# Up projections of the second layer's FFN: seven half-size products per chunk in place of eight, with sums of weights on POOL

## The chip, the cores and the metric

The kernel runs on 1 core of one Trainium2 chip. The metric is the device time of one execution in microseconds (us). The kernel before takes 1777.14 us (median of 3 runs, 1777.07 to 1779.08).

## What is computed

The program is a two-layer diffusion backbone on 512 latent and 256 context tokens. Each layer ends with a channel mixer (ConvGLU). The change concerns that of the second layer, which works on the 512 latent tokens only, in float32:

```python
def conv_ffn(h, w_up, conv_w, conv_b, w_down):
    gate, val = jnp.split(jnp.dot(h, w_up), 2, axis=-1)
    return jnp.dot(jax.nn.silu(dwconv(gate, conv_w, conv_b)) * val, w_down)

x = x + gt2 * conv_ffn(modulate(rmsnorm(x, norm2_g[layer]), sh2, sc2),
                       ffn_w_up[layer], ffn_conv_w[layer], ffn_conv_b[layer], ffn_w_down[layer])
```

The model width is 1024 and `w_up` is 1024 x 5632: a gate half and a value half of 2816 each. `dwconv` is a convolution over three neighbouring tokens.

## The kernel before

Activations lie with channels on the 128 partitions and tokens along the free axis. The 2816 channels of the FFN are done in 22 chunks of 128, the 1024 input channels are 8 slices `k` of 128. To keep float32 precision, each operand is split into a rounded high part and a remainder (`split`, L37: ACT writes the high part with a cast on L42, DVE subtracts on L43), and each product is made of three TensorE passes: high x high, low x high, high x low (`fm`, L76, whose matmuls are on L85). A weight tile of 128 x 1024 comes by DMA from SP's queue (`weights`, L59, L66) and is split once.

`ffn` (L295) does, for chunk `f` (`up`): 24 matmuls of 512 columns for the gate, 24 for the value; for the first four chunks each of these is two matmuls of 256 columns, one for each half of the tokens, so that work can start when the first half of the tokens is normalised. Then ACT scales the gate (L289), DVE adds the two neighbours from PSUM (L291, L292), ACT applies Silu (L323), DVE multiplies by the value in PSUM (L325), and `split` makes `ah` and `al`. After every four chunks, `down` (L330) multiplies with `w_down`: eight output slices of 12 matmuls (L343), each added into `X` by DVE (`xupd`, L378). `up` runs one chunk ahead of `down`.

Before the FFN, `norm` (L250) normalises X in two halves of 256 tokens: squares on ACT and sums on POOL and DVE, a reciprocal root in small DVE steps (L98), then for each `k` a DVE product `u` (L275), an ACT bias into `hh` (L277), and the remainder `hl` on DVE (even `k`, L283) or POOL (odd `k`, L280 and L281).

The engines run their instructions strictly in the order in which the scheduler of the framework put them. That order is fixed when the kernel is built. Weight tiles turn through a ring of buffers (`wtile`, L47): two for raw weights (`wr`) and three for each of `wh` and `wl` in this stage.

Of the kernel before, what the change touches and what calls it, by code (L numbers as in the profile page):

```python
# [21 lines left out]
KD = 8  # L22
NF = 22
# [5 lines left out]
def f32(ap):  # L29
    return ap.bitcast(F32)  # L30


class Kernel:
    def __init__(self, tc, ins, out):
        self.tc, self.nc, self.i, self.out = tc, tc.nc, ins, out
        self.turn = {}


# [255 lines left out]

    def ffn(self, l, X, hh, hl, pool, nt, extra, swap=None, after=None):  # L295
# [1225 lines left out]
```

## Time and profile before

| | |
|---|---|
| median of 3 runs | 1777.14 us |
| the profiled execution: its time, its span | 1778.27 us, 1776.3 us |
| PE busy in the span | 1685.1 us (95%) |
| DVE, ACT, POOL busy | 1246.0, 737.0, 327.2 us |
| chain that ended last, PE's share | 69% |
| second layer's FFN, first matmul to the end of the span | 1403.9 to 1776.3 us |
| first `down` of that FFN starts (five chunks are complete) | 1466.37 us |

Times in the trace count from the start of the span. A matmul row shows how long one instruction was in flight; neighbours overlap, so the rate is read from starts, or from a stretch of the chain divided by its count. DVE, ACT and POOL rows don't overlap within an engine by more than a tenth of a us or so.

### The profile page before, as it was taken

What the parts mean: (1) busy time and instruction counts of PE and PEld (TensorE: products, weight loads), DVE (VectorE), ACT (ScalarE), POOL (GpSimd) and SP (SyncE); (2) the same over time, 40 slices, a digit from 0 to 9 for tenths busy, and PEclk for the clock granted to TensorE, in tenths of its full rate; (3) what the DMA queues carried; (4) which work ended last, traced back from release to release, by engine and by line L of the source; (5) the groups of instructions that cost most, each with busy time, mean ns of one, the idle gap of its engine ahead of it and who ended that gap; (6) DMA issues with size and microseconds to landing.
All of it is one profiled execution on the core that took longest, in us unless ns stands there. A gap on an engine that the chain in (4) does not pass through costs nothing.

```text
span 1776.3 us, 25328 instructions
## 1 busy us (share of the span) xinstructions
PE 1685.1 (95%) x9622; PEld 1443.6 (81%) x9622; DVE 1246.0 (70%) x2285; ACT 737.0 (41%) x1369; POOL 327.2 (18%) x361
## 2 busy tenths in 40 slices
PE   6798889999999999999999998999999899999998
PEld 1587787888888888888888887788888798888887
DVE  5897898988878667585867548877778854544444
ACT  3333877888243222221222225645453442332231
POOL 4824445454040000000000005112020300000000
PEclk8898999999999999999999999999998999999999
DMA  8352000003525234242523222111112223322232
GB/s 276 112 169 64 10 11 7 19 1 132 166 82 191 96 130 143 95 157 81 166 96 131 72 75 76 52 48 49 60 36 95 72 96 98 104 95 95 96 98 91
DMA packets 68317, 166.28 MB, mean 94 GB/s; under 512 B 8290, under 2 KB 30818, under 8 KB 67810
## 3 DMA queue, kind: packets, MB, share of 16 engines
q1 hardware_dynamic: 68194, 164.66, 28.2%
q8 instruction: 76, 1.25, 0.3%
q14 instruction: 45, 0.37, 0.1%
q10 hardware_dynamic: 2, 0.01, 0.0%
HBM read 160.44 MB, written 4.20 MB: 93 GB/s over the span
## 4 chain that ended last, share of the span: by engine, by line
PE 69%; DVE 13%; ACT 7%; POOL 6%; issue 3%; DMA 1%; SPq 0%; POOLq 0%; ACTq 0%; DVEq 0%
PE psS L85 30%; PE psT L343 7%; PE psU L343 7%; PE psU L85 4%; PE psR L85 3%; PE psT L85 2%; PE psO L343 2%; PE psR L343 2%; PE S L424 1%; ACT p L432 1%; PE psO L469 1%; POOL hl L281 1%; DVE junk L138 1%; PE psR L95 1%; PE state L1190 1%
## 5 line engine op out<-in xcount | busy, mean ns | idle before, releaser
L85 PE MATMUL psS<-hl,wh 128*128 128x512 f32 (+1 forms) x992 | 347.2, 351 | 4.4 <-POOL hl L281 4.3
L85 PE MATMUL psS<-hh,wh 128*128 128x512 f32 (+1 forms) x992 | 346.3, 350 | 0.4 <-ACT hh L277 0.4
L85 PE MATMUL psS<-hh,wl 128*128 128x512 f32 (+1 forms) x992 | 346.0, 349 | 0.0
L42 ACT CAST wh<-wr 128x1024 fp32r<-128x1024 f32 (+2 forms) x187 | 193.5, 1036 | 349.1 <-PE psO L343 141.3
L43 DVE TENSOR_TENSOR wl<-wr,wh 128x1024 fp32r<-128x1024 f32 (+2 forms) x187 | 229.4, 1227 | 46.5 <-ACT wh L42 46.2
L85 PEld LDWEIGHTS psS<-hl,wh 128*128 128x128 f32 x992 | 186.4, 188 | 32.9 <-POOL hl L281 7.1
L85 PEld LDWEIGHTS psS<-hh,wh 128*128 128x128 f32 x992 | 186.5, 188 | 26.6 <-ACT hh L277 0.9
L85 PEld LDWEIGHTS psS<-hh,wl 128*128 128x128 f32 x992 | 186.5, 188 | 25.4
L291 DVE SCALAR_TENSOR_TENSOR y<-psS,fcw,y 128x511 f32<-128x511 f32 (+1 forms) x60 | 39.5, 658 | 145.6 <-ACT y L289 145.6
L261 POOL TENSOR_TENSOR sa<-sa,sq 128x256 f32<-128x256 f32 (+1 forms) x18 | 18.3, 1016 | 643.7 <-ACT sq L260 643.7
L138 DVE CUSTOM_DVE_ANT_0 y<-ar,cb 128x1024 f32<-128x1024 f32 x112 | 136.4, 1219 | 0.0
L289 ACT ACTIVATE y<-psS,fcb,fcw 128x512 f32<-128x512 f32 (+1 forms) x60 | 40.3, 706 | 207.2 <-PE psS L85 207.2
L378 DVE SCALAR_TENSOR_TENSOR X<-psU,mod,X 128x512 f32<-128x512 f32 (+1 forms) x69 | 47.9, 695 | 89.4 <-PE psU L343 78.9
L435 POOL TENSOR_SCALAR p<-p,rs 128x768 f32<-128x768 f32 (+1 forms) x96 | 73.9, 776 | 114.6 <-DVE rs L434 75.4
L138 DVE CUSTOM_DVE_ANT_0 junk<-ar,cb 128x1024 f32<-128x1024 f32 x64 | 84.0, 1312 | 0.5
L343 PE MATMUL psT<-ah,wh 128*128 128x512 f32 (+1 forms) x184 | 71.6, 389 | 2.2 <-DVE X L378 1.2
L343 PE MATMUL psU<-ah,wh 128*128 128x512 f32 (+1 forms) x184 | 71.4, 388 | 1.2 <-DVE X L378 1.2
L343 PE MATMUL psU<-ah,wl 128*128 128x512 f32 (+1 forms) x184 | 71.0, 386 | 0.0
L343 PE MATMUL psT<-ah,wl 128*128 128x512 f32 (+1 forms) x184 | 71.0, 386 | 0.0
L325 DVE TENSOR_TENSOR y<-y,psS 128x512 f32<-128x512 f32 (+1 forms) x60 | 34.1, 597 | 52.5 <-PE psS L85 52.4
L343 PE MATMUL psT<-al,wh 128*128 128x512 f32 (+1 forms) x184 | 70.9, 385 | 0.0
L343 PE MATMUL psU<-al,wh 128*128 128x512 f32 (+1 forms) x184 | 70.7, 384 | 0.0
(666 smaller groups left out, 4381.9 us busy)
## 6 DMA issues: line engine op xcount, KB each, us to landing
ar<-in_ada SPq DMA_DIRECT2D x88, 512.0 KB, 3.5
wr<-in_wup SPq DMA_DIRECT2D x88, 512.0 KB, 3.5
wr<-in_wdn SPq DMA_DIRECT2D x44, 512.0 KB, 3.4
pr<-in_adak SPq DMA_DIRECT2D x16, 256.0 KB, 4.3
wr<-in_w_out SPq DMA_DIRECT2D x8, 512.0 KB, 3.6
wr<-in_w_mqk SPq DMA_DIRECT2D x8, 512.0 KB, 3.5
wr<-in_w_mv SPq DMA_DIRECT2D x8, 512.0 KB, 3.6
wr<-in_w_mo SPq DMA_DIRECT2D x8, 512.0 KB, 3.4
```

What stands on the lines that cost most here:

```text
L42: nc.scalar.copy(hi, src)
L43: nc.vector.tensor_tensor(lo, src, f32(hi), op=SUB)
L85: nc.tensor.matmul(ps, a, b[:, k, x0:x0 + n], start=i == 0, stop=i == 3 * nk - 1)
L95: nc.tensor.matmul(ps, a[:, k, t * 128:(t + 1) * 128], b, start=i == 0, stop=i == 3 * nk - 1)
L138: nc.vector.tensor_tensor_reduce(out, raw, self.cb[:, c], 1.0, 0.0, MUL, ADD, self.mraw[l][:, n, c:c + 1])
L261: (nc.vector if k % 2 else nc.gpsimd).tensor_tensor(sa[k % 2], sa[k % 2], sq, op=ADD)
L289: nc.scalar.activation(y[:, t0:t0 + n], p, AF.Identity, bias=b, scale=w[1])
L291: nc.vector.scalar_tensor_tensor(y[:, t0 + 1:t0 + n], p[:, 0:n - 1], w[0], y[:, t0 + 1:t0 + n], op0=MUL, op1=ADD)
L325: nc.vector.tensor_tensor(y[:, t0:t0 + n], y[:, t0:t0 + n], p, op=MUL)
L343: nc.tensor.matmul(ps[:, 0:n], x[:, off:off + 128], y[:, t0:t0 + n], start=m == 0, stop=m == 3 * nf - 1)
L378: self.nc.vector.scalar_tensor_tensor(X[:, o, t0:t0 + n], ps[:, 0:n], self.mod[l][:, g0 + o, c:c + 1], X[:, o, t0:t0 + n], op0=MUL, op1=ADD)
L435: nc.gpsimd.tensor_scalar(p[:, 0:nk], p[:, 0:nk], r, 1.0, op0=MUL, op1=MUL)
```

## The change

The product of weights (two halves in output channels, gate and value, by two halves in input channels) with activations (two halves in input channels by two halves of tokens) is done in Winograd's form of Strassen's scheme. With the weights' quarters A11 (gate, k 0 to 3), A12 (gate, k 4 to 7), A21 and A22 (value), it takes seven products of 128 x 512 x 256 in place of eight.

- `norm_w` (in place of `norm` for this FFN) writes seven split operands: `B11` and `B21` from the first half of the tokens, `B22` from the second, and `T1` to `T4`, which are differences of the two halves. It keeps `h` of both halves in float32. Its sums are made of pairs of slices, 512 columns each.
- For each chunk, POOL makes four sums of weights of 128 x 512 (`S12`, `S43`: S1 = A21 + A22, S2 = S1 - A11, S4 = A12 - S2, S3 = A11 - A21). ACT and DVE split them as they do raw weights. Three tiles of 128 x 1024 (`A1`, `S12`, `S43`) and one of 128 x 512 (`A22`) are split per chunk, in place of two of 128 x 1024.
- Products accumulate in PSUM: `Y` (tags T and U) takes B11, T2, T3 and T4 in turn and is read in between; `Z` and `W` share a tile. Copies `p5`, `u2` and `g` go out on ACT, sums are added on DVE. The convolution reads its gate from SBUF (`g`).
- The value product for the second half of the tokens and the remainder `al` are done on POOL.
- A chunk is a generator of five stages; `ffn_w` interleaves stages of chunk f and f + 1. `down` uses the PSUM tags R and O.
- The ring has three more raw buffers and two more each for `wh` and `wl`, in the pool of this FFN (`we`), which takes up memory that the last part of the mixer and `norm_w` used.

```diff
     def wtile(self, tag, n, cols, dt):
...
+        if self.we and tag != "wr":
+            bufs += [(self.we, tag + "e"), (self.we, tag + "f")]
+        elif self.we:
+            bufs += [(self.we, tag + x) for x in "efg"]
...
+    def norm_w(self, pool, X, l, B, half, n, kept):
...
+        def low(name, k, src, eng):
+            eng.tensor_tensor(B[name][1][:, k], src, f32(B[name][0][:, k]), op=SUB)
+
+        for k in range(KD):
+            u = pool.tile([128, n], F32, tag="u", name="u", bufs=3)
+            nc.vector.scalar_tensor_tensor(u, X[:, k, t0:t1], s[:, k, 0:1], rb[:, 0:n], op0=MUL, op1=MUL)
+            sh = self.mod[l][:, 24 + k, 0:1]
+            nc.scalar.activation(h[:, k], u, AF.Identity, bias=sh)
+            if half == 0:
+                nm, kk = ("B11", k) if k < 4 else ("B21", k - 4)
+                nc.scalar.activation(B[nm][0][:, kk], u, AF.Identity, bias=sh)
+                low(nm, kk, h[:, k], nc.gpsimd if k % 2 else nc.vector)
+        if half == 0:
+            return
+        g = kept[0]
+        k2 = [(slice(a, a + 2), slice(a + 4, a + 6)) for a in (0, 2)]
+
+        for a, b in k2:
+            nc.vector.tensor_tensor(g[:, a], h[:, a], g[:, a], op=SUB)
+            nc.scalar.copy(B["T1"][0][:, a], g[:, a])
+            low("T1", a, g[:, a], nc.vector)
+        for a, b in k2:
+            nc.scalar.copy(B["B22"][0][:, a], h[:, b])
+            low("B22", a, h[:, b], nc.gpsimd)
+            nc.vector.tensor_tensor(h[:, a], h[:, b], h[:, a], op=SUB)
+            nc.vector.tensor_tensor(h[:, b], h[:, b], g[:, a], op=SUB)
+            nc.scalar.copy(B["T2"][0][:, a], h[:, b])
+            low("T2", a, h[:, b], nc.vector)
+        for a, b in k2:
+            nc.scalar.copy(B["T3"][0][:, a], h[:, a])
+            low("T3", a, h[:, a], nc.gpsimd)
+        for a, b in k2:
+            nc.vector.tensor_tensor(g[:, b], g[:, b], h[:, b], op=SUB)
+            nc.scalar.copy(B["T4"][0][:, a], g[:, b])
+            low("T4", a, g[:, b], nc.vector)
...
+        def prod(ps, w, x, first, last):
+            wh, wl = w
+            xh, xl = x
+            m = 0
+            for k in range(4):
+                for a, b in ((wh, xh), (wl, xh), (wh, xl)):
+                    nc.tensor.matmul(ps, a[:, k], b[:, k], start=first and m == 0, stop=m == 11, skip_group_check=True)
+                    m += 1
...
+        def chunk(f):
+            rg, rv = self.raw(i["wup"][l, f, 0], KD, 128), self.raw(i["wup"][l, f, 1], KD, 128)
+            A1 = self.halves(rg, KD, 128)
...
+            prod(Y, part(A1, 0), B["B11"], True, False)
+            prod(Z, part(A1, 1), B["B21"], True, True)
+            nc.scalar.copy(g[:, 0:n], Z)
+            nc.vector.tensor_tensor(g[:, 0:n], g[:, 0:n], Y, op=ADD)
+            yield
+            S = pool.tile([128, KD, 128], F32, tag="S12", name="S12", bufs=1)
+            nc.gpsimd.tensor_tensor(S[:, 0:4], rv[:, 0:4], rv[:, 4:8], op=ADD)
+            nc.gpsimd.tensor_tensor(S[:, 4:8], S[:, 0:4], rg[:, 0:4], op=SUB)
+            S12 = self.halves(S, KD, 128)
+            prod(W, part(S12, 0), B["T1"], True, False)
+            p5 = pool.tile([128, n], F32, tag="p5", name="p5", bufs=2)
+            nc.scalar.copy(p5, W)
+            yield
+            prod(Y, part(S12, 1), B["T2"], False, False)
+            S_ = pool.tile([128, KD, 128], F32, tag="S43", name="S43", bufs=1)
+            nc.gpsimd.tensor_tensor(S_[:, 0:4], rg[:, 4:8], S[:, 4:8], op=SUB)
+            nc.gpsimd.tensor_tensor(S_[:, 4:8], rg[:, 0:4], rv[:, 0:4], op=SUB)
+            S43 = self.halves(S_, KD, 128)
...
+            nc.scalar.copy(u2, Y)
+            prod(W, part(S43, 0), B["B22"], False, True)
+            nc.vector.tensor_tensor(g[:, n:nt], u2, W, op=ADD)
+            yield
+            A22 = self.halves(rv[:, 4:8], 4, 128)
+            prod(Y, part(S43, 1), B["T3"], False, False)
...
+            nc.vector.tensor_tensor(v2, p5, Y, op=ADD)
...
+            nc.scalar.activation(y, g, AF.Identity, bias=cb[:, f:f + 1], scale=cw[:, 1, f:f + 1])
+            for t0, m in segs:
+                nc.vector.scalar_tensor_tensor(y[:, t0 + 1:t0 + m], g[:, t0:t0 + m - 1], cw[:, 0, f:f + 1],
+                                               y[:, t0 + 1:t0 + m], op0=MUL, op1=ADD)
+                nc.vector.scalar_tensor_tensor(y[:, t0:t0 + m - 1], g[:, t0 + 1:t0 + m], cw[:, 2, f:f + 1],
+                                               y[:, t0:t0 + m - 1], op0=MUL, op1=ADD)
+            nc.scalar.activation(y, y, AF.Silu)
+            nc.gpsimd.tensor_tensor(y[:, n:nt], y[:, n:nt], v2, op=MUL)
+            yield
+            prod(Y, A22, B["T4"], False, True)
+            nc.vector.tensor_tensor(y[:, 0:n], y[:, 0:n], Y, op=MUL)
...
+            nc.scalar.copy(ah, y)
+            nc.gpsimd.tensor_tensor(al, y, f32(ah), op=SUB)
...
+        def up(f):
+            if f == 0:
+                upto(0, 1)
+                upto(1, 1)
+            upto(f, 3)
+            upto(f + 1, 1)
+            if f == 0:
+                upto(f + 1, 2)
+            upto(f, 4)
+            upto(f + 1, 2)
+            upto(f, 5)
...
-                ps = self.B("TU" if c == 0 or last else "RO")
+                ps = self.B("TU" if own and (c == 0 or last) else "RO")
...
-                    self.norm(NP, X, 1, 1, gh, gl, [(256 * half, 256 * half + 256, 0)])
+                    self.norm_w(NP, X, 1, B, half, 256, kept)
```

Two places of the fixed order matter below. The first is the start of the FFN. On ACT, right after the last `hh` of the second half of the tokens (L277), there stood before the scaling of chunk 0's gate; the weights of chunks 0 and 1 had been cast earlier:

```order
L277 ACTIVATE hh_13863<-u_14167,mod1_646 128x256
L277 ACTIVATE hh_13863<-u_14171,mod1_646 128x256
L289 ACTIVATE y_14293<-psS_14183,fcb1_654,fcw1_652 128x512
L42 CAST wh_14361<-wr_14359 128x1024
```

Now there stand the casts of B22 and T1 to T4 (`Ts` holds T1, T2 and T3), and behind them the cast of chunk 0's gate weights (`wh_14208`) and of its first sums (`wh_14281`):

```order
L325 ACTIVATE h_14145<-u_14167,mod1_646 128x256
L337 CAST Ts_13871<-h_13996 128x512 x2
L340 CAST B22h_13867<-h_14145 128x512
L347 CAST Ts_13871<-h_14145 128x512
L344 CAST Ts_13871<-h_14145 128x512
L347 CAST Ts_13871<-h_14145 128x512
L351 CAST T4h_13869<-h_13996 128x512
L344 CAST Ts_13871<-h_14145 128x512
L351 CAST T4h_13869<-h_13996 128x512
L43 CAST wh_14208<-wr_14204 128x1024
L43 CAST wh_14281<-S12_14278 128x1024
```

POOL likewise makes the remainders of B22 and T3 first (`L319`) and chunk 0's sums of weights behind them; DVE splits `wl_14209` behind its last T4. PE meets this at its 13th product matmul. `psU` is the first product of chunk 1, whose weights (`wh_14245`) were split early; `psT_14212` is the first of chunk 0:

```order
L393 MATMUL psU_14249<-B11h_13863,wl_14246 128x256
L393 MATMUL psU_14249<-B11l_13864,wh_14245 128x256
L315 MATMUL psO_14142<-ident_90,nwy_14130 128x128 x2
L393 MATMUL psT_14212<-B11h_13863,wh_14208 128x256
L393 MATMUL psZ_14213<-B21h_13865,wh_14208 128x256
L393 MATMUL psZ_14250<-B21h_13865,wh_14245 128x256
```

What moved: after 12 matmuls everything on PE stands behind `wh_14208`, which stands behind the casts of T4.

The second place is a chunk of the later FFN on DVE. Before, a chunk had six instructions there:

```order
L43 TENSOR_TENSOR wl_16292<-wr_16289,wh_16291 128x1024
L43 TENSOR_TENSOR al_16212<-y_16205,ah_16211 128x512
L291 SCALAR_TENSOR_TENSOR y_16277<-psS_16215,fcw1_652,y_16277 128x511
L292 SCALAR_TENSOR_TENSOR y_16277<-psS_16215,fcw1_652,y_16277 128x511
L43 TENSOR_TENSOR wl_16322<-wr_16319,wh_16321 128x1024
L325 TENSOR_TENSOR y_16277<-y_16277,psS_16216 128x512
```

Now it has ten, of which six read two operands from SBUF (four splits, and L435 and L437, whose gate `g` was in PSUM before):

```order
L44 TENSOR_TENSOR wl_16681<-S43_16677,wh_16680 128x1024
L426 TENSOR_TENSOR g_16443<-u2_16551,psZ_16442 128x256
L435 SCALAR_TENSOR_TENSOR y_16621<-g_16443,fcw1_652,y_16621 128x511
L437 SCALAR_TENSOR_TENSOR y_16621<-g_16443,fcw1_652,y_16621 128x511
L408 TENSOR_TENSOR g_16576<-g_16576,psU_16574 128x256
L44 TENSOR_TENSOR wl_16737<-wr_16568,wh_16736 128x512
L431 TENSOR_TENSOR v2_16619<-p5_16513,psT_16441 128x256
L44 TENSOR_TENSOR wl_16704<-wr_16699,wh_16703 128x1024
L443 TENSOR_TENSOR y_16621<-y_16621,psT_16441 128x256
L44 TENSOR_TENSOR wl_16764<-S12_16760,wh_16763 128x1024
```

What moved: on each chunk L431 (`v2`) and L443, for which PE waits before it may write `Y` again, now stand behind splits of the next chunk; and POOL, which had nothing to do here, has six instructions a chunk.

## Rows read from the trace of the kernel before

**Rows 1.** The chain that ended last, in order of time: start us, us, what.

```profile
1426.66 5.76 PE psR L85 x48
...
1466.37 2.72 PE psT L343 x12
...
1488.13 43.52 PE psS L85 x192
...
1749.25 10.89 PE psS L85 x48
1760.23 0.70 DVE y L325
...
1772.43 0.75 DVE X L378
```

**Rows 2.** Busy time by stretch: us, PE, PEld, DVE, ACT, POOL, PEclk, DMA share, GB/s.

```profile
1410.00:1414.00 4.00, 3.34 (x28) 3.34 (x29) 3.22 (x13) 0.00 (x0) 0.61 (x1) 1.00 0.65 168
1414.00:1422.00 8.00, 7.53 (x59) 6.95 (x58) 5.24 (x12) 4.21 (x9) 5.44 (x8) 1.00 0.14 49
...
1488.13:1531.65 43.52, 43.52 (x193) 36.04 (x193) 20.05 (x23) 15.18 (x19) 0.00 (x0) 1.00 0.27 89
```

**Rows 3.** Line 85, weight loads for psR: duration ns min/median/max, first and last start, forms.

```profile
L85 PEld LDWEIGHTS psR<-hh,wh x88: 187/188/192, 534.2 to 1454.8; 128*128 128x128 f32 x88
```

**Rows 4.** Groups by line and shape, DVE from 1400 us: busy us, mean ns | idle.

```profile
L43 DVE TENSOR_TENSOR wl<-wr,wh 128x1024 fp32r<-128x1024 f32 x65 | 80.0, 1232 | 13.4 <-ACT wh L42 13.4
...
L43 DVE TENSOR_TENSOR al<-y,ah 128x512 fp32r<-128x512 f32 x22 | 15.0, 684 | 0.7 <-ACT ah L42 0.7
L291 DVE SCALAR_TENSOR_TENSOR y<-psS,fcw,y 128x511 f32<-128x511 f32 x20 | 15.0, 750 | 69.3 <-ACT y L289 69.3
```

**Rows 5.** The same for ACT.

```profile
L42 ACT CAST wh<-wr 128x1024 fp32r<-128x1024 f32 x65 | 68.0, 1048 | 133.5 <-PE psU L343 85.1 <-PE psS L85 42.8 <-PE psR L85 4.9
...
L277 ACT ACTIVATE hh<-u,mod 128x256 fp32r<-128x256 f32 x16 | 7.2, 500 | 8.6 <-DVE u L275 8.6
```

**Rows 6.** Two lines of POOL, each by its own view: duration ns min/median/max.

```profile
L1168 POOL TENSOR_TENSOR Dl<-D,Dh x16: 1273/1291/2292, 1142.6 to 1350.6; 128x512 fp32r<-128x512 f32 x16
...
L281 POOL TENSOR_TENSOR hl<-v,hh x24: 726/752/2115, 505.7 to 1420.2; 128x256 fp32r<-128x256 f32 x16, 128x512 fp32r<-128x512 f32 x8
```

**Rows 7.** Instructions in order of time: start us, us, engine, line, what.

```profile
35.39 1.21 DVE L138 CUSTOM_DVE_ANT_0 junk<-ar,cb 128x1024 f32<-128x1024 f32 x1
...
35.42 6.37 POOL L206 TENSOR_TENSOR X<-X,rbs 128x256 f32<-128x256 f32 x4
...
36.54 0.68 DVE L173 TENSOR_SCALAR s<-mod,n0g 128x2 f32<-128x2 f32 x1
...
37.13 1.21 DVE L138 CUSTOM_DVE_ANT_0 junk<-ar,cb 128x1024 f32<-128x1024 f32 x1
```

**Rows 8.** The same view around the second half of the norm.

```profile
1402.59 1.26 DVE L275 SCALAR_TENSOR_TENSOR u<-X,s,psO 128x256 f32<-128x256 f32 x3
...
1410.02 1.67 DVE L43 TENSOR_TENSOR wl<-wr,wh 128x1024 fp32r<-128x1024 f32 x1
...
1414.16 1.26 DVE L275 SCALAR_TENSOR_TENSOR u<-X,s,psO 128x256 f32<-128x256 f32 x3 [0.63 <-PE psO L272]
1414.67 1.31 ACT L277 ACTIVATE hh<-u,mod 128x256 fp32r<-128x256 f32 x3 [6.35 <-DVE u L275]
```

**Rows 9.** Busy time by stretch at the end of the mixer, columns as above.

```profile
1337.00:1340.00 3.00, 0.90 (x5) 0.72 (x6) 3.00 (x7) 2.23 (x4) 0.00 (x0) 0.76 0.97 415
1340.00:1344.00 4.00, 4.00 (x21) 4.00 (x20) 2.99 (x5) 0.26 (x2) 0.00 (x0) 0.50 0.32 131
1344.00:1347.00 3.00, 3.00 (x12) 2.71 (x12) 2.51 (x8) 0.26 (x1) 0.00 (x0) 0.50 0.37 126
1347.00:1350.00 3.00, 3.00 (x14) 2.72 (x14) 2.48 (x6) 2.08 (x4) 0.66 (x1) 0.70 0.02 5
```

**Rows 10.** PE in order of time in the same place.

```profile
1339.62 0.45 PE L1190 MATMUL state<-V,kwh 128*128 128x130 f32 x1 [1.48 <-DVE num L1227]
```

More of the change, by code (lines that the diff above doesn't have):

```diff
@@ L36, in __init__ @@
         self.turn = {}
+        self.we = None
     def split(self, hi, lo, src, scale=None):
@@ L292, in conv, with raw, halves @@
             nc.vector.scalar_tensor_tensor(y[:, t0:t0 + n - 1], p[:, 1:n], w[2], y[:, t0:t0 + n - 1], op0=MUL, op1=ADD)
-    def ffn(self, l, X, hh, hl, pool, nt, extra, swap=None, after=None):
+    def raw(self, src, n, cols):
+        t = self.wtile("wr", n, cols, F32)
+        self.nc.sync.dma_start(t, src)
+        return t
+    def halves(self, src, n, cols):
+        hi = self.wtile("wh", n, cols, F32R)
+        lo = self.wtile("wl", n, cols, F32R)
+        self.split(hi, lo, src)
+        return hi, lo
@@ new lines, in ffn_w, with go, upto @@
+    def ffn_w(self, l, X, B, pool, nt):
+        a = {}
+        make = self.up_w(l, B, pool, nt, a)
+        ch = {}
+        def go(f, n=1):
+            for _ in range(n):
+                next(ch[f], None)
+        stage = {}
+        def upto(f, st):
+            if f >= NF:
+                return
+            if f not in ch:
+                ch[f] = make(f)
+            while stage.get(f, 0) < st:
+                go(f)
+                stage[f] = stage.get(f, 0) + 1
+        def up(f):
[9 more added lines that the diff above has]
+            upto(f, 5)
+        self.ffn(l, X, None, None, pool, nt, [], up=up, a=a)
@@ L296, in ffn @@
+    def ffn(self, l, X, hh, hl, pool, nt, extra, swap=None, after=None, up=None, a=None):
         nc, i = self.nc, self.i
@@ L299, in ffn, with up_plain @@
         cw, cb = self.fcw[l], self.fcb[l]
-        a = {}
+        own = up is None
+        a = {} if own else a
         ytile = lambda: pool.tile([128, D], F32, tag="y", name="y", bufs=3)[:, 0:nt]
-        def up(f):
+        def up_plain(f):
             alone = f < 4 and f % 2 == 1
@@ L368, in ffn @@
             while done < min(NF, fs[-1] + 2):
-                up(done)
+                (up or up_plain)(done)
                 done += 1
@@ L1392, in build @@
             hp = tc.alloc_tile_pool(name="h3", bufs=1, reuse_waits="tile")
-            gh = hp.tile([128, KD, NL], F32R, name="hh")
-            gl = hp.tile([128, KD, NL], F32R, name="hl")
+            B = {nm: [hp.tile([128, 4, NL // 2], F32R, tag=nm + e, name=nm + e) for e in "hl"]
+                 for nm in ("B11", "B21", "B22", "T4")}
+            z = HP.tile([128, KD, T], F32R, tag="hl", name="Ts").rearrange("p k t -> p (k t)").rearrange(
+                "p (j k t) -> p j k t", j=6, k=4)
+            B.update({nm: [z[:, 2 * j], z[:, 2 * j + 1]] for j, nm in enumerate(("T1", "T2", "T3"))})
+            kept = {}
             with tc.tile_pool(name="o1", bufs=1, reuse_waits="tile") as OP, \
```

46 lines of the change are left out of this document (45 added, 1 removed).

## The prediction, made before the changed kernel ran

> **What bounds the kernel now.** I read first the chain that ended last, in order of time. In the second layer's FFN it is PE without a break: 192 matmuls of 512 columns in 43.52 us, 226.7 ns each, then the next `down` [rows 1]. The first four chunks use 256 columns, 48 in 5.76 us, 120 ns each [rows 1]. The busy time by stretch then shows what the others do meanwhile: in the stretch from 1488 us DVE is busy for 20 of 43.5 us and POOL for none, at the full granted clock [rows 2]. So PE sets the end, and less work for PE is worth its full price as long as PE finds its operands ready. Third, the start of this FFN, where PE was already fed by a chain of DVE, ACT and POOL [rows 8], yet busy for 7.5 of 8 us just before 1422 [rows 2]. Fourth, places where DVE and POOL work at once [rows 7], since the change puts much on both.
>
> **PE's work.** Before: 4 chunks x 96 x 0.120 + 18 x 48 x 0.2267 = 46.1 + 195.8 = 241.9 us. Now every chunk has 7 x 12 = 84 matmuls of 256 columns: 22 x 84 x 0.120 = 221.8 us. That is 20.1 us less, not an eighth, because a half-width matmul costs 120 ns and not 113. A weight load takes 188 ns [rows 3], though such matmuls follow each other at 120 ns: loads overlap. The Trainium skill ("TensorE: Matmul & The Clock Gate", section "The mechanism") says that loads overlap with matmuls in flight only if they go to another row group; by that each of these, on all 128 rows, would have to wait for its load, but this trace disagrees with its 120 ns.
>
> **DVE and POOL get in each other's way.** While POOL ran four sums of 128 x 256 in 6.37 us, 1.59 each [rows 7], against 0.73 alone [rows 6], DVE read two SBUF operands in its own instructions, and a DVE step on two elements took 0.68 us [rows 7]. They alternate: one DVE instruction of 1.21 us and one of POOL of 0.73 have a period of 1.74 us (35.39 to 37.13) [rows 7], 0.9 of the sum of their durations. I count a "shared" instruction (DVE with two SBUF operands, every sum on POOL) at 0.9 of its duration and let none overlap. The Trainium skill ("SBUF — State Buffer", section "Who interferes with whom") calls it an exclusive lock, held for the whole instruction. The trace agrees that one waits for the other; by the rule's letter the factor is 1.0.
>
> Shared work per chunk now, with 1.23 us for a split, 0.68 for half of one, 0.70 for a neighbour sum (between 0.68 and 0.75) [rows 4], 1.29 and 0.73 for POOL's 512 and 256 columns [rows 6]: DVE 3 x 1.23 + 0.68 + 2 x 0.70 = 5.8, POOL 5 x 1.29 + 0.73 = 7.2, in all 13.0, x 0.9 = 11.7 us. PE needs 84 x 0.120 = 10.1. So within four chunks the shared work is the longer of the two; during a `down` (21.76 us) it is the shorter and some is made in advance.
>
> **The start.** The second half's `u` steps began at 1414.16, behind two splits in DVE's queue, one of 1.67 us [rows 8]; these now stand later, but ACT has two activations per slice in place of one in the first half. I take 1411 (bounds 1410 and 1414). Eight steps paced by ACT, 0.44 each (1.31 for three [rows 8]), end at 1414.6. Then DVE has twelve shared steps of 512 columns up to the last source of T4: 12 x 0.68 = 8.2, and between them POOL's four remainders and up to two sums of weights at 1.16: 4.6 to 7. That is 1429. The cast of T4 (0.6) and then, next in ACT's order, of chunk 0's weights (1.05 [rows 5]) end at 1431; the split's second half waits behind two more steps of T2 and T4 and POOL's turns: 1433. PE has 12 matmuls until then, whose operands are ready by 1410; it stands still for over 20 us where before it was nearly full [rows 2].
>
> From 1433 to the first `down` PE has 30 products of 1.44 us (chunks 0 to 3 and three of chunk 4, one being done): 43.2 us. After a gap of some 2 us (PE idle 1.48 us before 1339.62, with three transposes just ahead of that [rows 9, 10]) the granted clock was 0.50, the 1.2 GHz level, from 1340 to 1347 and 0.70 to 1350 [rows 9]: about 9 us at half speed, 4.5 lost. Together 1480.7. The other way round, the shared work between 1428 and that `down`: DVE the two late steps 1.4, three splits and a half for chunk 0 and so on through chunk 4 (18.7), four for `w_down` 4.9, eight neighbour sums 5.6; POOL 16 sums of weights 20.6 and four times 2.02 for the value product and `al`. Sum 59.3, x 0.9 = 53.4: 1481.4. Both give 1481. Before, the first `down` began at 1466.37 [rows 1], four products of a chunk further on.
>
> **From there on.** Before, 309.9 us remained. Now: four products 5.8, 17 chunks x 10.08 = 171.4, five `down`s and a half 119.7, and the 5.2 us by which the end is longer than its matmuls: 302.1. At the very end chunk 21 has nothing beside it: PE waits for `v2`, and `al` takes 1.29 on POOL in place of 0.68 [rows 4, 6], while the product with Y is half as wide: +1.7, bounds 0 and 3. Between two `down`s the shared work is 24.9 on DVE (ten splits and three halves, four for `w_down`, eight sums) and 23.6 on POOL, 48.4 in all, x 0.9 = 43.6 against PE's 40.3. The excess is 3.3; part can slip under the first columns of the `down`, and part of PE's waits for `v2` come on top. No row shows the balance; the bounds are 0 (all made in advance) and 8.1 (factor 1.0). I take 2.5, nearer the factor that the row gives, four times: 10.
>
> **The sum.** 1481 + 302.1 + 1.7 + 10 = 1794.8 for the end of the span, against 1776.3 (the last DVE step at 1772.43 [rows 1] and the copy out behind it): +18.5 on the profiled execution's own 1778.27, so 1796.8. The median of the runs is 1.1 lower than that execution: 1795.7, and I say 1795.
>
> SP's queue carries the same bytes, with five raw buffers in place of two; the transfer for chunk 0 waits for the mixer's last matmuls, at about 1402, and lands long before 1429, so it costs nothing. ACT's added copies (three of 256 columns, one and a half casts, some 3 us a chunk) fit in its idle time (15 of 43.5 us busy [rows 2]). Clock drops inside the FFN are not counted: PE's gaps there would be short.
>
> **Rivals.**
> 1. *The two engines run side by side and PE restarts early.* For it: `u` steps that read PSUM show no slowing [rows 8]; against it, the 1.59 us sums. Without any blocking, 1414.6 + 8.2 + 1.7 + 1.2 = 1425.7, no clock loss, + 43.2 = 1468.9, + 302.1 + 0 to 1.7: 1771 to 1773, in time 1772 to 1774, faster by about 4 us. It decides if PE's first product of chunk 0 runs before 1426.
> 2. *The start costs what I say, but after it PE alone sets the pace*, with the clock up at once: 1433 + 43.2 + 302.1 + 1.7 = 1780, time 1781, or up to 3 us less with an earlier start.
> 3. *Full exclusion through every group of four chunks*, as the lock rule has it, from rows at factor 1.0: first `down` at 1430 + 59.3 = 1489, then 8.1 per group: 1489 + 302.1 + 1.7 + 32 = 1825, time 1826. The period of 1.74 us speaks against the letter of it, DVE's strict order (a late split delays `v2`, and with it PE) for it.
> 4. *Weight loads bind* at 188 ns: 22 x 84 x 0.068 = +126 us. The 120 ns rows are against it.
> That the change doesn't cut PE's work can be ruled out: 84 matmuls a chunk stand in the order.
>
> **How the numbers follow.** Forecast (1785 to 1806) 0.59; rival 2 (1777 to 1785) 0.15, a little over half of it within 0.2%; rival 1 0.10; rival 3 (1806 to 1826) 0.14; rival 4 0.02. The range from 1777 to 1813 leaves out rivals 1 and 4 and half of rival 3. About 0.2% (3.6 us) is what a measurement can tell from no change: faster 0.10, same 0.09, slower 0.81.
>
> **What would show it.** Right: matmuls of L393 starting 120 ns apart; PE idle from about 1411 until about 1430, ended by ACT's cast of `wh`; a granted clock near 0.5 for some us behind it; POOL's sums of 512 columns at 1.5 to 2.5 us and splits of DVE at well over 1.23; first `down` near 1481. Wrong: PE's gap under 15 us, POOL's sums near 1.29 with DVE busy, or gaps in later groups of over 8 us or none.

## The result, and the profile after

The changed kernel takes 1841.06 us (median of 4 runs, 1838.86 to 1846.16) against 1778.11 of the kernel before (4 runs, 1777.07 to 1779.30): ratio 1.0358, 95% interval 1.0335 to 1.0381. It is slower, as forecast, but by 63 us, not by 18, and lies outside the range. The profiled execution took 1838.86 us, its span is 1837.1 (before: 1778.27 and 1776.3).

The chain that ended last, in order of time, shows where each `down` begins (start us, us, what):

```profile
1494.16 2.52 PE psR L535 x11
...
1567.95 2.52 PE psR L535 x11
...
1641.21 2.52 PE psR L535 x11
...
1789.38 2.52 PE psR L535 x11
```

Before, five `down`s began from 1466.37 to 1727.49, 65.28 apart [rows 1]; now they are 73.8 apart. The 60.8 us of span are: first `down` 27.8 later, four groups 4 x (73.8 - 65.28) = 34.1, and from the fifth `down` on 1.1 less (47.7 against 48.8).

The 27.8 are too few by 7.4 us. The first `u` of the norm ran at 1395.18, where before it ran at 1402.59 [rows 8], behind work that the change leaves alone; the first layer's first `down` also began at 590.5 us in place of 596.1, and in the traces of all runs it begins between 590.5 and 598.4. So two traces can stand some us apart before they come to the changed code. Counted from the first `u`, the first `down` came after 99.0 us in place of 63.8, 35.2 later. Times of two traces are therefore compared below from a place that both share, where it matters.

Busy time by stretch, kernel after (us, PE, PEld, DVE, ACT, POOL, granted clock, DMA share, GB/s): three pieces of the start, one `down`, the products up to the next `down`, and four pieces around one gap.

```profile
1410.00:1418.00 8.00, 0.00 (x0) 0.00 (x0) 6.85 (x7) 2.55 (x5) 6.72 (x5) 0.50 0.00 0
1418.00:1424.00 6.00, 1.36 (x5) 1.14 (x5) 6.00 (x4) 2.98 (x5) 5.73 (x4) 0.50 0.00 0
1424.00:1430.00 6.00, 4.54 (x25) 4.46 (x25) 3.76 (x4) 0.88 (x1) 3.16 (x2) 0.58 0.28 87
1567.95:1589.60 21.65, 21.65 (x99) 17.93 (x98) 9.91 (x14) 4.31 (x5) 3.85 (x3) 1.00 0.31 90
1589.60:1641.21 51.61, 44.62 (x338) 43.30 (x337) 39.34 (x40) 25.31 (x39) 36.30 (x22) 0.93 0.26 85
1622.00:1625.00 3.00, 2.45 (x21) 2.24 (x19) 2.96 (x2) 0.54 (x2) 2.92 (x3) 1.00 0.00 0
1625.00:1628.00 3.00, 0.67 (x3) 0.67 (x4) 3.00 (x5) 1.83 (x3) 1.97 (x2) 0.83 0.01 3
1628.00:1631.00 3.00, 3.00 (x18) 3.00 (x18) 0.89 (x2) 0.64 (x1) 1.06 (x1) 0.60 0.76 225
1631.00:1634.00 3.00, 3.00 (x27) 3.00 (x27) 2.03 (x2) 2.16 (x4) 1.81 (x1) 1.00 0.36 125
```

Against [rows 2]: between two `down`s PE stands still for 7.0 of 51.6 us and has a mean clock of 0.93, where it had neither gaps nor a lower clock. In the `down` POOL works for 3.85 us only; after it for 36 of 52.

The costliest groups of DVE, kernel after, 1430 to 1760 us (busy us, mean ns | idle before); they answer to [rows 4]:

```profile
L44 DVE TENSOR_TENSOR wl<-wr,wh 128x1024 fp32r<-128x1024 f32 x34 | 55.2, 1624 | 7.0 <-ACT wh L43 6.9
L44 DVE TENSOR_TENSOR wl<-S,wh 128x1024 fp32r<-128x1024 f32 x38 | 51.5, 1354 | 28.4 <-ACT wh L43 25.9 <-PE psZ L393 1.5 <-issue 0.9
L435 DVE SCALAR_TENSOR_TENSOR y<-g,fcw,y 128x511 f32<-128x511 f32 x19 | 27.7, 1456 | 12.4 <-ACT y L433 12.4
...
L426 DVE TENSOR_TENSOR g<-u,psZ 128x256 f32<-128x256 f32 x19 | 7.8, 412 | 8.0 <-PE psZ L393 7.0 <-ACT wh L43 1.0
```

and of POOL, which answer to [rows 6]:

```profile
L411 POOL TENSOR_TENSOR S<-wr 128x512 f32<-128x512 f32 x19 | 33.4, 1757 | 20.4 <-DMA wr<-in_wup 14.9 <-DVE wl L44 5.5
...
L447 POOL TENSOR_TENSOR al<-y,ah 128x512 fp32r<-128x512 f32 x18 | 32.6, 1812 | 22.0 <-ACT ah L446 22.0
```

A split takes 1.35 to 1.62 us in place of 1.23, a neighbour step 1.46 in place of 0.75, a sum on POOL 1.53 (L420) to 1.76 (L411) in place of 1.29. L426 and DVE's other short steps, which take one operand from PSUM and one from SBUF, take 0.41, the same as where POOL does nothing (0.41 to 0.42 in e3 below).

What PE waited for between 1494 and 1760 us (total, times, longest):

```profile
PE psU L393 <- DVE y L443: 8.1, 4, 2.0
PE psU L393 <- DVE v L431: 7.4, 3, 2.9
PE psT L393 <- DVE v L431: 5.2, 4, 2.1
PE psZ L393 <- ACT g L407: 4.6, 4, 1.1
```

The first three are short steps of 0.41 us, which come late in DVE's queue. At the start (in order of time: start us, us, engine, line, what, and in brackets the idle time before it), POOL and DVE take turns in the T steps, and PE restarts on ACT's cast of chunk 0's weights:

```profile
1395.18 1.27 DVE L323 SCALAR_TENSOR_TENSOR u<-X,s,psO 128x256 f32<-128x256 f32 x3
...
1411.38 1.74 DVE L343 TENSOR_TENSOR h<-h 128x512 f32<-128x512 f32 x1 [1.15 <-POOL B22l L319]
1412.53 1.71 POOL L319 TENSOR_TENSOR Ts<-h,Ts 128x512 fp32r<-128x512 f32 x1
1413.04 1.75 DVE L342 TENSOR_TENSOR h<-h 128x512 f32<-128x512 f32 x1
...
1422.64 0.58 PE L393 MATMUL psT<-B11h,wh 128*128 128x256 f32 x1 [18.69 <-ACT wh L43]
...
1425.54 0.58 PE L393 MATMUL psT<-B11h,wl 128*128 128x256 f32 x1 [1.47 <-DVE wl L44]
```

### The profile page after: what moved, and what is told of

Read it like the earlier page. It is cut to its first block, busy times and chain, and to the rows that moved or that the text cites. A ratio compares the mean times of both kernels' runs of the same rounds, so it can differ in the third digit from the quotient of the medians.

```text
span 1837.1 us, 26989 instructions
## 1 busy us (share of the span) xinstructions
PE 1682.9 (92%) x10222; PEld 1469.5 (80%) x10222; DVE 1355.5 (74%) x2383; ACT 798.4 (43%) x1497; POOL 543.6 (30%) x485
## 4 chain that ended last, share of the span: by engine, by line
PE 60%; DVE 18%; ACT 9%; POOL 7%; issue 5%; DMA 1%; POOLq 0%; SPq 0%; DVEq 0%; ACTq 0%
PE psS L90 18%; PE psR L535 5%; PE psO L535 5%; PE psU L90 4%; DVE wl L44 4%; PE psT L535 3%; PE psU L535 3%; PE psR L90 2%; PE psT L393 2%; PE psU L393 2%; ACT wh L43 2%; PE psT L90 2%; PE S L616 2%; PE psO L661 1%; PE psZ L393 1%
## 5 line engine op out<-in xcount | busy, mean ns | idle before, releaser
L43 ACT CAST wh<-wr 128x1024 fp32r<-128x1024 f32 (+3 forms) x187 | 183.5, 985 | 290.1 <-PE psO L535 154.1
L44 DVE TENSOR_TENSOR wl<-wr,wh 128x1024 fp32r<-128x1024 f32 (+3 forms) x187 | 238.9, 1278 | 43.0 <-ACT wh L43 42.6
L90 PE MATMUL psS<-hl,wh 128*128 128x512 f32 (+1 forms) x640 | 216.7, 340 | 2.1 <-POOL hl L286 2.1
L90 PE MATMUL psS<-hh,wh 128*128 128x512 f32 (+1 forms) x640 | 216.2, 338 | 0.4 <-ACT hh L282 0.4
L90 PE MATMUL psS<-hh,wl 128*128 128x512 f32 (+1 forms) x640 | 216.2, 338 | 0.0
L90 PEld LDWEIGHTS psS<-hl,wh 128*128 128x128 f32 x640 | 120.3, 188 | 18.0 <-POOL hl L286 3.7
L90 PEld LDWEIGHTS psS<-hh,wh 128*128 128x128 f32 x640 | 120.3, 188 | 15.1 <-ACT hh L282 0.6
L90 PEld LDWEIGHTS psS<-hh,wl 128*128 128x128 f32 x640 | 120.3, 188 | 14.4
L44 DVE TENSOR_TENSOR wl<-S,wh 128x1024 fp32r<-128x1024 f32 x44 | 59.2, 1346 | 32.2 <-ACT wh L43 29.7
L619 DVE TENSOR_REDUCE nm<-S 128x1 f32<-128x768 f32 x64 | 60.2, 946 | 3.9 <-PE S L616 3.5
```

The costliest lines, as they stand in the source:

```text
L43: nc.scalar.copy(hi, src)
L44: nc.vector.tensor_tensor(lo, src, f32(hi), op=SUB)
L90: nc.tensor.matmul(ps, a, b[:, k, x0:x0 + n], start=i == 0, stop=i == 3 * nk - 1)
L619: nc.vector.tensor_reduce(nm, s[:, 0:nk], axis=AX.X, op=MAX, negate=True)
```

## Experiments

Three theories for the 8.5 us per group. **A**: DVE's instructions on two SBUF operands and POOL's exclude each other, so POOL's work lengthens DVE's queue, and what PE waits for comes late. **B**: the chain raw load, sum, split, product, with one buffer each for S12 and S43, makes the products late, whatever engine makes the sums. **C**: DVE's own added work is too much. The table has all runs; the kernel before measured 1778.1 to 1779.3 beside them. "Group" is the mean time from one `down` to the next; PE alone needs 28 x 1.44 + 21.76 = 62.1.

| run | us | ratio to before, 95% | group |
|---|---|---|---|
| the change | 1841.1 | 1.0358 (1.0335 to 1.0381) | 73.8 |
| e1_no_sums | 1794.7 | 1.0090 (1.0073 to 1.0107) | 64.4 |
| e2_sums_unread | 1849.6 | 1.0402 (1.0381 to 1.0422) | 75.1 |
| e3_no_pool | 1781.6 | 1.0016 (1.0001 to 1.0031) | 62.1 |
| e4_act_drains | 1837.7 | 1.0326 (1.0301 to 1.0352) | 71.6 |
| e5_tail_dve | 1839.1 | 1.0352 (1.0328 to 1.0376) | 72.4 |
| e6_sums_dve | 1800.7 | 1.0131 (1.0113 to 1.0150) | 65.8 |
| e8_deep | 1849.8 | 1.0408 (1.0388 to 1.0429) | 74.3 |
| e10_idle_sums | 1837.9 | 1.0323 (1.0304 to 1.0342) | 72.1 |
| e14_two_idle | 1805.0 | 1.0152 (1.0130 to 1.0175) | 66.4 |
| e11_idle_copies | 1799.2 | 1.0106 (1.0089 to 1.0124) | 65.3 |
| e12_low_dve | 1780.9 | 1.0008 (0.9997 to 1.0019) | 62.1 |
| e7_start | 1780.5 | 1.0013 (1.0002 to 1.0025) | 62.1 |
| e9_start2 | 1778.9 | 1.0000 (0.9988 to 1.0013) | 62.1 |
| e13_start3 | 1778.8 | 1.0001 (0.9988 to 1.0015) | 62.1 |

### Sums left out, and sums made but not read (e1, e2)

```diff
-            S = pool.tile([128, KD, 128], F32, tag="S12", name="S12", bufs=1)
-            nc.gpsimd.tensor_tensor(S[:, 0:4], rv[:, 0:4], rv[:, 4:8], op=ADD)
-            nc.gpsimd.tensor_tensor(S[:, 4:8], S[:, 0:4], rg[:, 0:4], op=SUB)
-            S12 = self.halves(S, KD, 128)
+            S12 = self.halves(rv, KD, 128)
```

and the same for S43 with `rg`; e2 has only the last line of it, so POOL's sums stay.

> Left out: the four sums of weights on POOL in each chunk; the splits of S12 and S43 read the raw values of rv and rg instead. Everything else, the seven products among it, stays. Measured for the changed kernel: 73.8 us from one down to the next, of which PE alone would need 62.1, and 1841 us in all. Theory A (DVE and POOL hold each other up, which stretches DVE's queue, so the PSUM reads that PE waits for come late): with only two POOL instructions left in a chunk the splits fall back from 1.55 to about 1.25 us, groups take 62 to 66 us, the start gains 4 to 8 us: 1795 to 1805. Theory B (the order of dependences: a sum is made late because its buffer or its source is late, and its split and product with it): the same fall, 1795 to 1805. Theory C (DVE's own added work, or PE's narrow products, set the pace): groups stay at 71 to 74 us, 1832 to 1843.

> POOL makes all four sums of weights as in the changed kernel, but no split reads them: the splits of S12 and S43 read the raw values of rv and rg. What is left out is the use of the sums, and with it the chain sum, split, product. Theory A (the two engines hold each other up while both work): the sums still run beside DVE, so groups stay at 71 to 75 us and the time at 1825 to 1843. Theory B (the chain through the sums makes the products late): groups fall to 62 to 66 us and the time to 1795 to 1805, as without sums.

Without sums 1794.7, about what A and B both said, so C is out; with sums that no split reads 1849.6. So it is not the chain through the sums: cutting it gave nothing, taking POOL's work away gave 46. That e2 is 8.6 slower than the change, and above A's range as well, stays unexplained. In e2 DVE's splits are at least as slow as in the change (groups of DVE, 1430 to 1760 us):

```profile
L44 DVE TENSOR_TENSOR wl<-wr,wh 128x1024 fp32r<-128x1024 f32 x71 | 119.3, 1700 | 25.9 <-ACT wh L43 23.7 <-PE psZ L393 2.0
```

One part of B is left in e2: POOL still reads the raw weights and so holds their buffers. The run with useless sums below takes that away too.

### All of POOL's work on DVE (e3)

```diff
-            nc.gpsimd.tensor_tensor(S[:, 0:4], rv[:, 0:4], rv[:, 4:8], op=ADD)
+            nc.vector.tensor_tensor(S[:, 0:4], rv[:, 0:4], rv[:, 4:8], op=ADD)
```

and so for the other three sums, for `y` times `v2` and for `al`.

> The four sums, the product y times v2 and the remainder al of each chunk run on DVE; POOL does nothing in the chunks. The result is the same. Theory A: DVE's instructions return to the lengths they have alone (split 1.23, sum of 512 columns 0.68, of 256 about 0.35 to 0.40), so DVE needs 5.8 + 4 x 0.68 + 0.68 + 0.4 + four PSUM steps of about 0.4 = 11.2 us a chunk against PE's 10.1, less than the 11.7 at factor 0.9 and the longer real one: groups of 66 to 70 us, time 1808 to 1828, faster than the changed kernel by 13 to 33 us although DVE does more. Theory B (the chain through the sums, whatever engine makes them): groups 72 to 76, 1835 to 1850. Theory C (DVE's own work is the bound, POOL relieves it): DVE gets 3.8 us more per chunk, groups 80 to 88, 1870 to 1900.

1781.6 us: 59.5 less than the change, better than A's range (1808 to 1828), and less than e1, which does 88 instructions fewer. The groups are PE's alone: the `down`s come 62.06 apart. The chain, then the stretch between two of them, then DVE's groups from 1430 to 1760 us:

```profile
1485.45 2.75 PE psR L535 x12
...
1547.51 2.75 PE psR L535 x12
...
1609.57 2.75 PE psR L535 x12
```

```profile
1569.30:1609.40 40.10, 40.10 (x336) 39.93 (x336) 37.96 (x59) 24.94 (x39) 0.00 (x0) 1.00 0.30 93
```

```profile
L44 DVE TENSOR_TENSOR wl<-S,wh 128x1024 fp32r<-128x1024 f32 x44 | 53.7, 1220 | 8.9 <-ACT wh L43 8.8
...
L435 DVE SCALAR_TENSOR_TENSOR y<-g,fcw,y 128x511 f32<-128x511 f32 x21 | 15.7, 745 | 0.0
...
L420 DVE TENSOR_TENSOR S<-wr,S 128x512 f32<-128x512 f32 x22 | 15.1, 687 | 0.3
```

All of DVE's instructions have their lengths of before, and PE has no gap and the full clock. B and C fall: the chain is the same and DVE has more to do. DVE works for 38.0 of 40.1 us between two `down`s. In the change it worked for 39.3 of 51.6, with 40 instructions in place of 59: giving a third of its instructions to POOL had relieved DVE of nothing. A sum takes 0.69 on DVE and 1.29 on POOL by itself [rows 6]; if only one of them can run at a time, POOL is no help but the dearer place.

### One part moved alone (e5, e6)

In e5 the tail (`y` times `v2`, `al`) goes to DVE and the sums stay on POOL; in e6 the other way round.

> Only the tail of a chunk (y times v2, 256 columns, and the remainder al, 512 columns) goes from POOL to DVE; the four sums of weights stay on POOL. The same result. If the instructions that exclude each other simply add up and set the pace between two downs (changed kernel: 5.8 us on DVE and 7.2 on POOL per chunk by their durations alone, 13.0, four times 52.0, and 52.1 us measured between the end of one down and the next), then a chunk has 5.8 + 0.68 + 0.42 + 4 x 1.29 = 12.06, and a group takes 21.7 + 48.2 = 70 us, 3.8 less than 73.8: 1841 - 4 x 3.8 - 3 = 1823, bounds 1817 to 1829. If only the number of POOL's sums and their late sources matter (order, buffers), groups stay at 73 to 75 us: 1834 to 1846.

> The other part: the four sums of weights go to DVE, y times v2 and al stay on POOL. The same result. By the same addition a chunk has 5.8 + 4 x 0.68 = 8.5 on DVE and 2.02 on POOL, 10.5 in all, so 42.2 between two downs against PE's 40.3: groups of 62 to 65 us, and 1781 (all on DVE) + 4 x 2 + 2 = 1791, bounds 1783 to 1798. If what counts is that PE's next product waits for DVE alone, whose queue now holds the sums too: groups of 70 us and more, 1820 to 1840.

e6 came out just above its upper bounds (1800.7, bound 1798; groups 65.8, bound 65): two instructions per chunk left on POOL still cost 19 us against e3. What PE waits for there, 1494 to 1760 us:

```profile
PE psT L393 <- DVE v L431: 7.8, 8, 1.3
PE psU L393 <- DVE v L431: 1.8, 4, 0.5
```

The chain that ended last in e6 also runs through POOL's product itself (L440, 3.08 us from 1605.17), so e6 alone doesn't part the exclusion from the chain through the tail.

e5 is a miss: groups fell by 1.4, not by 3.8, and the time by 2 us, less than the runs of either kernel spread. Adding up durations alone doesn't give the pace (more on this below).

### PE freed from DVE's late steps (e4), and more raw buffers (e8)

```diff
-            nc.vector.tensor_tensor(v2, p5, Y, op=ADD)
+            t3 = pool.tile([128, n], F32, tag="t3", name="t3", bufs=2)
+            nc.scalar.copy(t3, Y)
+            nc.vector.tensor_tensor(v2, p5, t3, op=ADD)
```

and so for the product after T4 (e4). In e8 the ring of raw weights has two more tiles, `ah` and `al` one less each.

> After T3 and after T4 ACT copies the Y accumulator (256 columns) to SBUF, and DVE adds and multiplies from the copies later; so PE's next product needs no instruction of DVE's queue to have run. ACT gets two copies of about 0.4 us more per chunk, DVE reads two SBUF operands in these two steps. The result is the same. Theory A1 (DVE has time enough, but stands in a strict order, so that v2 and y come late by up to 2.9 us; the gaps of 7.4 us a group and the half clock behind them, 3.6, are all there is): groups 63 to 67 us, time 1800 to 1815. Theory A2 (the shared work of DVE and POOL as a whole takes more than PE's time, and PE only waits for it at these places): PE waits elsewhere (weights, S12 and S43 splits), groups 71 to 75 us, 1832 to 1845.

> The changed kernel (sums and tail on POOL) with seven buffers for raw weights in place of five, and ah and al with seven in place of eight to make room. The same result. In the changed kernel POOL makes one sum during a down and waits 12 us for a raw load. If it is the raw buffers that keep sums out of the down, POOL works 3 to 6 us more in it and groups fall to 67 to 71 us: 1812 to 1831. If the single buffers of S12 and S43 or those of the split weights hold them back as well, groups stay at 73 to 75: 1836 to 1848.

e4 gained 3 us, and the intervals of the two ratios overlap: A1's 1800 to 1815 is missed, A2's range holds. PE's wait only changes its name (1494 to 1760 us): ACT's copies stand in ACT's order behind steps that wait in turn, for DVE's neighbour steps (the third line) and for PE. Two DVE steps also read both operands from SBUF now, which adds to the shared work.

```profile
PE psT L393 <- ACT t L432: 10.9, 3, 3.7
PE psZ L393 <- ACT g L407: 4.9, 4, 1.4
ACT y L441 <- DVE y L439: 32.4, 14, 3.9
```

In e8 the wait for raw loads in the `down` is gone, and a longer one has its place: POOL's waits before (48.8 us for raw loads and 33.9 for splits, four times each) and now:

```profile
POOL S L420 <- DVE wl L44: 87.6, 4, 21.9
```

So one more limit, the splits that a sum's buffer waits for, keeps the sums out of the `down`: groups stay at 74.3, in the second forecast's range; the time, 1849.8, is just above it. No run has two buffers for S12 and S43, so what sums made during the `down` would give stays open.

### Useless work on POOL (e10, e14, e11)

The e3 kernel, with four (e14: two) instructions per chunk that nobody reads; e11 uses one operand.

```diff
+            junk = pool.tile([128, nt], F32, tag="junk", name="junk", bufs=1)
+            for _ in range(4):
+                nc.gpsimd.tensor_tensor(junk, g, g, op=ADD)
```

e11: `nc.gpsimd.tensor_scalar(junk, g, 1.0, None, op0=MUL)`.

> The kernel with nothing on POOL in the chunks (1781.6), and in each chunk four useless sums on POOL (g plus g, 128x512, into a tile that nobody reads). The same result; nothing waits for these sums, and no raw weight is held by them. Theory A (while POOL reads two operands, DVE's instructions with two SBUF operands wait, and the other way round): 88 x 1.29 = 113 us of POOL's work fall beside a DVE that is already full between two downs (40 of 40 us), so part of it is paid: each chunk has 9.9 + 4 x 1.29 = 15.1 us of it, in the down some 10 us are free; groups of 70 to 80 us, time 1815 to 1860. Theory B (only the chain through the sums and their buffers matters): 1779 to 1785.

> The kernel with nothing on POOL in the chunks and two useless sums per chunk on POOL in place of four. The same result. With four, 88 sums cost 56.3 us, 0.64 each, about half of a sum's 1.29. If every sum beside a full DVE costs the same, 44 cost 28: 1805 to 1815. If there is slack that takes the first ones (DVE's waits, the down), less than proportional: 1783 to 1800.

> As the run before, but the four useless instructions of each chunk read one operand (g times 1.0, 128x512) in place of two. The same result. If it is any work of POOL in SBUF that holds DVE up (bandwidth, semaphores), the time is nearly that of the useless sums: 1810 or more. If it needs a second operand, or DVE and POOL can work side by side with such instructions: 1779 to 1790. The trace's row of before for such an instruction (L280, 836 ns for 256 columns and more) says that it isn't shorter on POOL than a sum.

88 useless sums bring back nearly the whole loss: 1837.9, 56.3 over e3 (of 59.5), 0.64 us each; 44 cost 23.4, 0.53 each. There is no chain and no raw buffer in it, and no instruction in the trace waits for one of these sums. What they do is in DVE's rows: from 1425 us on, its 285 instructions of the FFN on two SBUF operands take 295.6 us in e10 against 238.5 in e3, 57.1 more, and in e14 28.5 more. DVE had little room between two `down`s (38.0 of 40.1 us), so nearly all of it is time lost. DVE in order of time in e10:

```profile
1539.38 0.68 DVE L420 TENSOR_TENSOR S<-wr,S 128x512 f32<-128x512 f32 x1
1539.98 1.53 DVE L450 TENSOR_TENSOR al<-y,ah 128x512 fp32r<-128x512 f32 x1
1541.43 1.52 DVE L435 SCALAR_TENSOR_TENSOR y<-g,fcw,y 128x511 f32<-128x511 f32 x1
1542.88 1.52 DVE L421 TENSOR_TENSOR S<-wr 128x512 f32<-128x512 f32 x1
1544.33 0.41 DVE L408 TENSOR_TENSOR g<-g,psU 128x256 f32<-128x256 f32 x1
```

POOL ran four sums from 1539.60 to 1545.30, beside all but the first row. There each DVE instruction on two SBUF operands takes 1.52 in place of 0.68 or 0.75; the one that reads PSUM keeps its 0.41. DVE's starts are 1.45 apart; a useless sum, which reads one tile twice, takes 1.04 at least by itself, and not the 1.29 that I had in the text of e14.

The Trainium skill ("SBUF — State Buffer", section "Who interferes with whom") says that such a DVE instruction contends with POOL instructions that read SBUF, and that one with at most one SBUF input does not. Here the trace agrees: 1.52 and 0.41.

e11 lies far below that, between the two ranges that I had: 17.6 us over e3, 0.2 per instruction, though POOL's one-operand form is the longer one (line 443 of e11; ns min/median/max):

```profile
L443 POOL TENSOR_SCALAR junk<-g x88: 1488/1798/3477, 1440.4 to 1782.3; 128x512 f32<-128x512 f32 x88
```

The Trainium skill ("SBUF — State Buffer", section "Summary: rules for kernel authors") says that where DVE has two SBUF inputs and POOL's instruction reads SBUF, the second to issue is blocked until the first has finished. This trace doesn't bear that out for one operand on POOL: in e11 DVE's product of 256 columns took 0.74 on average and never more than 0.86 (0.42 in e3), beside instructions of 1.5 us and over. So for one operand the hold is partial.

### The start (e12, e7, e9, e13)

All on top of e3. e12 puts the norm's last remainders on DVE; e7 also loads, sums and splits chunk 0's first weights (and A1 of chunk 1) during and before the norm; e9 writes their first stage into the norm; e13 adds S43 of chunk 0. Of e7:

```diff
+            rg, rv = self.raw(self.i["wup"][1, 0, 0], KD, 128), self.raw(self.i["wup"][1, 0, 1], KD, 128)
+            A1 = self.halves(rg, KD, 128)
+            nc.vector.tensor_tensor(S[:, 0:4], rv[:, 0:4], rv[:, 4:8], op=ADD)
+            nc.vector.tensor_tensor(S[:, 4:8], S[:, 0:4], rg[:, 0:4], op=SUB)
...
-            low("T3", a, h[:, a], nc.gpsimd)
+            low("T3", a, h[:, a], nc.vector)
```

> The kernel with nothing on POOL in the chunks, and the four remainders of T3 and B22 in the norm's second half on DVE as well. The same result. If POOL's four remainders (up to 2.3 us each there, 0.68 on DVE) hold DVE's T steps up, T4's last remainder ends 1 to 3 us before 1428.2 and the time falls to 1778 to 1781; if DVE's four more steps cost what they save: 1781 to 1784.

> The kernel with nothing on POOL in the chunks, and in addition another start: chunk 0's weights are loaded, A1(0) split and S12(0) summed during the mixer's last matmuls, A1(1) and S12(0) are split in the middle of the norm, and the remainders of T3 and B22 run on DVE. There is one buffer less for ah and al each. The same result. With all on DVE PE loses nothing after the start, so what is left is the start: PE idle for 16.6 us up to 1425 and half clock until 1434. If the start is a matter of order, PE begins chunk 0 at 1409 to 1413 instead of 1425, has four products until T1 is ready, and the first down begins 8 to 14 us earlier than 1485.5: time 1765 to 1774, faster than the kernel before (1778) by 4 to 13. If the norm's own chain on DVE and ACT is the bound, and work put into it delays it by as much: 1776 to 1783.

> The kernel with the other start, where PE ran three early products and then stood for 14.7 us because ACT's copy of Z (g) stood behind the casts of T in ACT's queue. Now the first stage of chunks 0 and 1 (copy of Z, sum with Y) is written into the norm, ahead of the T steps; g's two tiles lie in the pool that outlives the norm. The same result. If that order is what held PE: the wait on g is gone, PE does the fourth early product and T1 of chunk 0 from about 1421, the first down begins 3 to 7 us before 1482.3, time 1773 to 1778. If DVE's whole work up to the splits of chunk 0 and 1 (busy 9.9 of 10 us from 1420 to 1430) is the bound: no change, 1779 to 1782.

> The kernel with the second form of the start, in which PE still waited 4.6 us for ACT's cast of S43(0) after T2, and in addition S43 of chunk 0 summed during the mixer's last matmuls and split behind the T2 steps, ahead of T3 and T4; ah and al with six buffers. The same result. If order is what is left of the start: the wait is gone, the clock comes back some us earlier, 1770 to 1776, faster than the kernel before (1779) by 3 to 9. If DVE's whole work up to there is the bound, T3 and T4 come as much later and PE waits for them: 1777 to 1781.

In e7, e9 and e13 PE's first matmuls of chunk 0 came even earlier than hoped (1404.7 to 1408.2 us; in e3 PE's wait ended at 1428.5), but the first `down` hardly moved: it began at 1485.3 in e3, 1481.1 in e12, 1482.1 in e7, 1482.8 in e9, 1483.8 in e13. Counted from the first matmul of the mixer's last product, ahead of all that these runs change, that is 139.4, 138.6, 136.9, 137.5 and 136.2 us: 1 to 3 gained on e3, where e7 was to gain 8 to 14, and the kernel before needs 121.0. The stretch from 1410 to 1480 suggests why. In e13:

```profile
1410.00:1480.00 70.00, 58.62 (x422) 55.15 (x422) 67.68 (x117) 45.56 (x80) 3.69 (x3) 0.91 0.21 69
```

DVE is busy for 66.9 to 68.6 of these 70 us in all five. The theory that the start is mainly a matter of order falls: the large waits that were removed (16.6 us for the cast in e3, 14.7 for `g` in e7, 4.6 for S43 in e9) left others behind (5.8 and 6.0 us for ACT's cast of T1 in e9 and e13). That DVE's work is the bound there fits, but no run takes work off DVE at the start to show it. No version beats the kernel before by more than its interval; e9 and e13 are level with it.

## Why the prediction was right or wrong

**PE's work: right.** 120 ns per matmul, 20.1 us less in all; e3 shows it, groups of 62.06 against 65.28. ACT's added work fits by its busy time (25.3 of 51.6 us), and weight loads didn't bind (rival 4).

**The start: right up to PE's restart, wrong behind it.** PE's gap was there (18.7 us, ended by ACT's cast, then 1.5), and DVE and POOL took turns. The restart at 1425.5 looks 7.5 us early, but this execution was 7.4 us ahead before it came to the changed code; by the trace of before it is 1432.9, where I had 1433. In the same way rival 1's sign, a first product of chunk 0 before 1426, is met by the number alone (1422.6, by the trace of before 1430). One slip in counting: before the first `down` PE has 37 products of this FFN, not 31. That moves 8.6 us from what remains to the time before (1489.6 in place of 1481) and cancels in the sum. From the first `u` the forecast then has 87.0 us to the first `down`, and 99.0 were measured: 12.0 late. That is PE standing still behind its restart, for 12.2 of 68.6 us, 11.0 of them for `v2`, where my sum had its products one after the other (the stretch, then the waits in it):

```profile
1425.54:1494.16 68.62, 56.41 (x441) 54.65 (x442) 53.92 (x53) 33.88 (x53) 49.76 (x30) 0.97 0.31 96
```

```profile
PE psU L393 <- DVE v L431: 5.5, 2, 2.9
PE psT L393 <- DVE v L431: 5.5, 3, 3.6
```

**The failing step: PE's waits for DVE's late steps, above all "between two `down`s".** I had "3.3 ... I take 2.5 ... four times: 10", nothing for such waits ahead of the first `down`, and "clock drops inside the FFN are not counted: PE's gaps there would be short". Measured were 73.8 - 62.1 = 11.7 each, four times 47. The forecast of the span missed by 42.3 us: 36.8 of these groups, the 12.0 ahead of the first `down`, 0.9 at the end, less the 7.4 by which this execution was ahead. That the total misses by little more than the groups alone is luck. The mechanism was the one named, and the runs show it (e3, e10); the size was off for three reasons:

1. The shared work itself was sized about right, but it can't be packed. One DVE instruction of 0.68 us and one of POOL of 1.29 have a period of 1.66 (1411.38 to 1413.04), 0.84 of their sum, where I had 0.9. In the stretch from 1589.6 to 1641.2 a shared instruction is under way for 44.2 of 51.6 us, and I had 43.6. In the other 7.4 us there is none: for 2.0 DVE runs its steps from PSUM with POOL idle, and for 5.4 neither engine works. I had put that at nothing. DVE stands idle for 12.3 us in all there, 8.6 of them for ACT's casts of weights and scalings of gates, which wait for PE and POOL in turn (up to 5.0 and 3.7 us). Which of these waits would go by another order was not shown.
2. I let part of the excess slip under the `down`. POOL worked 3.85 us there, about one sum less than I had counted on (28.8 us a group less 23.6), first waiting for raw loads, then for splits (e8).
3. PE's longer gaps cost more than themselves. After the gap of 2.9 us before 1627.33 the granted clock was 0.60 from 1628 to 1631, and after one of 2.0 us before 1606.07 it was 0.57 from 1606 to 1610. Over the stretch PE stood for 7.0 us and ran at 0.93, another 3.6.

Rival 3 had the right kind (8.1 a group, 1826), and still too small, for the same reasons. Its chance of 0.14 was too low: the strict order of DVE's queue, which I named in its favour, is what turns a long queue into PE's gaps. Rival 2 (the start only) is what e3 became once POOL was out of the way. None of the signs that I had named as wrong came: PE's gaps were 7.0 us a group, under the 8 that I had set, and the clock and the waits ahead of the first `down` had no sign of their own.

## What to carry to other kernels

Before moving elementwise work on two SBUF operands from DVE to POOL, look at what DVE does at that time: if it is such work too, the two take turns. Here a sum costs 0.69 us on DVE; on POOL it takes about 1.0 us of the time that the two share (a pair of 0.68 and 1.29 takes 1.66). Nearly the whole loss was undone by moving it back (1841.1 to 1781.6, before 1778.1). Where PE reads results through a strict queue, don't compare sums of busy time alone: allow for what can't be packed, and for the clock that PE loses in each gap.

## What was not expected of the hardware

- A useless sum on POOL that nothing waits for costs the program 0.53 to 0.64 us beside a full DVE (e14, e10); the one-operand form, longer by itself (1.49 us at least against 1.04), costs 0.2 (e11).
- A gap of 2.9 us in dense PE work was followed by a granted clock of 0.60 over three microseconds, and full clock behind it; after a gap of 1.1 us before 1598.07 the clock stayed at 1.00 (1600 to 1606).
- The traces of two kernels with the same work up to there lie 7.4 us apart when they come to the changed code (1395.18 and 1402.59).
